# A transformer block in split fp32: the two output-gate projections as one seven-product unit, with weight sums made by accumulating transfers

## The chip, the cores and the metric

The kernel runs on one core of a Trainium2 chip. The metric is device time in microseconds (us) of one execution; lower is better. A core has TensorE (PE, matrix multiplication; its weight loads are listed as PEld), VectorE (DVE), ScalarE (ACT), GpSimd (POOL) and SyncE (SP). SP, ACT and POOL can also issue transfers (DMA). Each engine works through its own queue in order and waits there for results of the others.

## What is computed

The reference is one decoder layer with 512 tokens and a model width of 1024, in float32. The part that matters here is the combined input projection, cut into sections, and the gated linear attention (GLA) that uses two of them:

```python
h = layer_norm(x, ln_in_g, ln_in_b)
q_g, k_g, v_g, r_g, a_lr, q_lat, kv_lat, gate_logits = jnp.split(h @ w_in, offsets, axis=-1)
...
o_gla = gla_chunked(q_g, k_g, v_g, log_a)
o_gla = rms_norm(o_gla, gla_norm_g)
y_gla = (o_gla * jax.nn.silu(r_g)) @ w_o_gla
...
y_mla = merge_heads(o_mla) @ w_o_mla
return (g_gla * y_gla + g_mla * y_mla) @ w_out
```

The output gate `r_g` is 512 tokens x 1024 columns, a product of `h` (512 x 1024) with 1024 columns of `w_in`. A squared-ReLU MLP and two more layer norms follow.

## The kernel before

**Split operands.** Each float32 operand of a matmul is held as two parts: a rounded "hi" part (type fp32r) and the rest, "lo". One product is then three matmuls: hi x hi, hi x lo, lo x hi. `split` (L104) makes the parts: ACT copies to hi, DVE subtracts for lo. For weights `pump` (L157) does the same at L180 (ACT) and L181 (DVE), 128x1024 elements at a time, which is two 128-row slices of the contraction by 512 columns.

**The weight stream.** `plan` (L138) appends weight pieces to one list, `stream`, in the order of use. `pump(i)` is called before piece i is used. It issues loads from SP up to two pieces ahead (L168, into the three buffers "wraw") and splits pieces up to `ahead` ahead (1, unless the entry says otherwise). An entry can say where its parts go (`home`): "w" is the pair of double buffers "whi"/"wlo", "a" is two buffers of the general pool. An entry with `src` in place of `dmas` is not loaded by `pump`; it takes a buffer that other code has filled.

**Buffers.** `A` (L72) gives 4 KB a partition: "C" has 8 such buffers, the general tag "A" 24. `B` (L76) gives 2 KB and has 22. `MM` gives one of four accumulators for the large products, `PX` one of four for everything else. A tile that finds no free buffer waits for one.

**Products.** `gemm_fm` (L221) and `gemm_tm` (L246) loop over k, the eight 128-row slices of the contraction, and within a slice over the accumulators. After each k they call `tick`, which lets the first few of a list of generators (`active`, spawned with `spawn`) issue their next piece of work: the latents, the score levels of GLA, the GLA output. A generator's work thereby stands between the large products on every queue. The framework takes the traced order as priority and places each instruction when it finds it ready, so engines may run ahead of the traced order where their operands allow.

**The order.** After the layer norm comes the latent section `lat`, then q, k, and then `ORDER` (L288): r 0, v 0, g 0, r 1, v 1, g 2, the MLA query part, g 1, g 3, and again the query part. The index of r and v is the half of 512 columns; half 0 serves heads 0 and 1. `proj_r` (L599) computes one half: 8 slices x 4 token tiles x 3 matmuls of 128x512, at L264, L265 and L266, which `proj_v` and others use too. For each token tile it forms x (1 + tanh(x / 2)) with one Tanh on ACT (L604) and one DVE operation (L607), which both read the accumulator. `proj_v` (L588) splits its result instead.

**Background generators.** `latents2` (L548) normalises and transposes the latents. `gla_levels` (L637) builds the scores of one head in about twelve steps, alternating between DVE (L649, L685), ACT (L667) and small matmuls, with totals and products on POOL (L624, L632, L635). `gla_out` (L735) starts for a head once its scores, its value half and its r half are there. `WID` says how many generators a tick advances: 2 during q and k, 3 afterwards.

**An example elsewhere in the kernel.** The second product of the MLP (`win_f2`, L1170) already uses seven products for each 2 x 2 block of matrices, with sums of weights made on DVE (`win_sums`), and adds its results to rows in SBUF by accumulating transfers from POOL (L1216). Its weights are loaded by POOL too (L1131).

## Time and profile before

| | us |
|---|---|
| median of three runs | 880.97 (880.94 to 882.45) |
| the profiled execution | 881.23 |
| its span, first to last instruction | 879.5 |

A line of a group of instructions reads: line, engine, operation, output <- inputs, shapes, count, then busy time in us, the mean of one in ns, and the idle time of the engine just ahead of them with what ended it. A line of the timeline begins with the start and the length in us. In the table of stretches each engine has its busy time and, in brackets, the number of its instructions; then come the clock granted to PE (1.00 is full), the share of time that the DMA engines were busy, and GB/s. A line of waits reads: who waited, for whom, total us, how often, longest.

### The profile page before, as it was taken

Reading aid. Unit: us, or ns where it says so; the run is one execution under the profiler, and the core shown is the slowest. Engines: PE = TensorE matmul, PEld = TensorE weight load, DVE = VectorE, ACT = ScalarE, POOL = GpSimd, SP = SyncE. Lnnn points to the kernel's source line nnn. Section 1 sums busy time; section 2 is a strip of 40 time slices with the busy share of each in tenths; the row PEclk is TensorE's granted clock in tenths of the full one; section 3 lists DMA queues with packets and bytes.
Section 4 is the critical chain, followed back from the end, with each engine's and each line's share of the span. In section 5 each row is a group of like instructions: output and inputs, shape, how many; then the busy total and the mean of one; then the engine's idle time right before and its main releaser. Section 6 shows DMA issues by size and latency. Waiting matters only on the chain. (4 is left out here: it accounts for less than half of the span.)

```text
span 879.5 us, 11469 instructions
## 1 busy us (share of the span) xinstructions
PE 861.5 (98%) x4336; PEld 735.0 (84%) x4336; DVE 562.8 (64%) x925; ACT 443.3 (50%) x766; POOL 141.4 (16%) x184
## 2 busy tenths in 40 slices
PE   5999999999999999999999999999999999999996
PEld 5988888888888888888988888988888888888885
DVE  6934774648455244557876797886567646754697
ACT  5547462556344333345654414565357546644662
POOL 2204330211011010000000013004400520242023
PEclk9999999999999999999999999999999999999998
DMA  7513223222232323112306628006940990398075
GB/s 224 158 49 93 75 73 96 73 72 57 81 87 81 90 60 110 47 55 60 103 27 262 192 75 284 1 0 170 291 114 27 263 256 29 63 302 209 1 183 104
DMA packets 63415, 101.13 MB, mean 115 GB/s; under 512 B 7777, under 2 KB 31764, under 8 KB 63360
## 3 DMA queue, kind: packets, MB, share of 16 engines
q1 hardware_dynamic: 48400, 64.04, 23.7%
q0 software_dynamic: 13040, 32.71, 15.6%
q10 hardware_dynamic: 1920, 3.66, 1.2%
q8 instruction: 34, 0.56, 0.3%
q14 instruction: 21, 0.17, 0.1%
HBM read 82.56 MB, written 3.67 MB: 98 GB/s over the span
## 5 line engine op out<-in xcount | busy, mean ns | idle before, releaser
L181 DVE TENSOR_TENSOR wlo<-wraw,whi 128x1024 fp32r<-128x1024 f32 (+2 forms) x102 | 116.3, 1140 | 148.1 <-ACT whi L180 142.0
L231 PE MATMUL mm<-h,whi 128*128 128x512 f32 x416 | 162.4, 391 | 0.0
L232 PE MATMUL mm<-h,whi 128*128 128x512 f32 x416 | 162.3, 390 | 0.0
L233 PE MATMUL mm<-h,wlo 128*128 128x512 f32 x416 | 156.4, 391 | 0.0
L180 ACT ACTIVATE whi<-wraw 128x1024 fp32r<-128x1024 f32 (+2 forms) x102 | 99.8, 978 | 110.3 <-PE mm L232 51.5
L233 PEld LDWEIGHTS mm<-h,wlo 128*128 128x128 f32 x416 | 78.0, 188 | 16.2
L231 PEld LDWEIGHTS mm<-h,whi 128*128 128x128 f32 x416 | 78.1, 188 | 15.7
L232 PEld LDWEIGHTS mm<-h,whi 128*128 128x128 f32 x416 | 78.2, 188 | 15.5
L1216 POOL DMA_DIRECT2D res<-ev x54 | 47.7, 994 | 237.1 <-ACT ev L1214 190.9
L265 PE MATMUL mm<-wlo,h 128*128 128x512 f32 x128 | 50.5, 395 | 0.0
L266 PE MATMUL mm<-whi,h 128*128 128x512 f32 x128 | 50.1, 391 | 0.0
L264 PE MATMUL mm<-whi,h 128*128 128x512 f32 x128 | 48.2, 395 | 0.0
L1281 ACT ACTIVATE relu<-mm 128x512 f32<-128x512 f32 x32 | 18.8, 595 | 57.2 <-PE mm L233 57.2
L359 POOL TENSOR_TENSOR mv<-mv,mhalf 128x1 f32<-128x1 f32 x4 | 4.1, 1034 | 208.6 <-DVE mv L358 208.6
L649 DVE TENSOR_TENSOR qk<-qk,tot 128x512 f32<-128x512 f32 x28 | 20.1, 719 | 19.9 <-ACT M L667 19.7
L180 ACT ACTIVATE xh<-wraw 128x1024 fp32r<-128x1024 f32 (+1 forms) x20 | 19.0, 960 | 26.9 <-PE mm L266 15.3
L667 ACT ACTIVATE M<-qk 128x256 f32<-128x256 f32 x56 | 24.0, 456 | 16.9 <-DVE qk L649 16.7
L181 DVE TENSOR_TENSOR wlo<-wq,whi 128x1024 fp32r<-128x1024 f32 x15 | 18.3, 1223 | 20.4 <-ACT whi L180 20.4
L266 PEld LDWEIGHTS mm<-whi,h 128*128 128x128 f32 x128 | 24.1, 188 | 4.8
L265 PEld LDWEIGHTS mm<-wlo,h 128*128 128x128 f32 x128 | 24.1, 188 | 4.6
L264 PEld LDWEIGHTS mm<-whi,h 128*128 128x128 f32 x128 | 23.9, 188 | 4.6
L1214 ACT ACTIVATE ev<-mm 128x512 f32<-128x512 f32 x20 | 11.9, 600 | 28.8 <-DMA res<-ev 23.9
(405 smaller groups left out, 2215.1 us busy)
## 6 DMA issues: line engine op xcount, KB each, us to landing
wraw<-in_w_in_dram SPq DMA_DIRECT2D x40, 512.0 KB, 3.6
wraw<-in_w_ff_dram SPq DMA_DIRECT2D x32, 512.0 KB, 7.1
wq<-in_w_ff_dram POOLq DMA_DIRECT2D x32, 512.0 KB, 10.0
res<-ev POOLq DMA_DIRECT2D x54, 256.0 KB, 8.6
wraw<-in_w_o_gla_dram SPq DMA_DIRECT2D x8, 512.0 KB, 3.7
wraw<-in_w_o_mla_dram SPq DMA_DIRECT2D x8, 512.0 KB, 3.4
wraw<-in_w_out_dram SPq DMA_DIRECT2D x8, 512.0 KB, 4.3
wraw<-in_w_in_dram SPq DMA_DIRECT2D x8, 360.0 KB, 4.6
```

Of the source, the lines that this page charges most:

```text
L180: st["ins"] = act(hi[:, :nk, :n], raw[:, :nk, :n], AF.Copy)
L181: vtt(lo[:, :nk, :n], raw[:, :nk, :n], f(hi[:, :nk, :n]), op=ALU.subtract)
L231: mm(o, hi[:, c], xh, start=first, stop=False)
L232: mm(o, hi[:, c], xl, start=False, stop=False)
L233: mm(o, lo[:, c], xh, start=False, stop=last)
L264: mm(o, xh, hi[:, :n], start=opens, stop=False, skip_group_check=share)
L265: mm(o, xh, lo[:, :n], start=False, stop=False, skip_group_check=share)
L266: mm(o, xl, hi[:, :n], start=False, stop=last, skip_group_check=share)
L649: vtt(new, new, view(tot, o + 1, -1, 2, 0, s), op=ALU.mult)
L667: act(packed(M, s, i), half_lr(qk, s, i), AF.Copy)
L1216: nc.gpsimd.dma_start(res[tt + t][:, j * T:(j + 1) * T], e, accum_op=ALU.add)
L1281: act(r, ps, AF.Relu)
```

## The change

The two halves of r become one unit. Write `hT` (h transposed, split) as 2 x 2 blocks, tokens 0 to 255 and 256 to 511 by slices 0 to 3 and 4 to 7, and the r columns of `w_in` likewise (W11, W12 above W21, W22). Seven block products replace eight; each is 4 slices x 2 token tiles x 3 matmuls of 128x512.

Four products use a sum of weight blocks. `T1` = W12 + W11; `T2` adds W22 to it in place, `T3` adds W12 to the buffer of W22, and `T4` adds W21 to T2. The first block of each is loaded, and every further one is added, by a transfer of 512 KB that POOL issues (with `accum_op`); a block is two such transfers. W11 and W21 are loaded from SP as before. All 14 half blocks go through `pump`, split two pieces ahead, with homes alternating between "w" and "a".

Four products use a sum of token blocks (`S1` to `S4`): a new generator, `r_sums`, makes them from hi and lo of `hT` with DVE additions and subtractions, and splits them. It is spawned ahead of q. The results come together in four tiles `R`: ACT copies an accumulator out with the wanted sign (`put`), and later DVE adds or subtracts the final accumulator and the gate function follows (`last`). Some products continue in an accumulator of an earlier one, which saves additions.

`ORDER` becomes r, v 0, v 1, g 0, g 2, and the rest as before; `finish(t_lat2)` follows r, as it followed r 0.

```diff
-    ORDER = (("r", 0), ("v", 0), ("g", 0), ("r", 1), ("v", 1), ("g", 2), ("qr", 0), ("g", 1), ("g", 3), ("qr", 1))
+    ORDER = (("r", 0), ("v", 0), ("v", 1), ("g", 0), ("g", 2), ("qr", 0), ("g", 1), ("g", 3), ("qr", 1))
+    RPH = ("T1", "11", "22", "T2", "21", "T3", "T4")
+    RAHEAD, RHOME = 2, "wawawawawawaww"
...
-            PL["r", i] = plan("w_in", C_R + i * T, T)
+            for n, op in enumerate(RPH):
+                for hf in range(2):
+                    PL["r", n, hf] = len(stream)
+                    if op in ("11", "21"):
+                        plan("w_in", C_R, T, 4 * (op == "21") + 2 * hf, 4 * (op == "21") + 2 * hf + 2)
+                    else:
+                        stream.append({"src": lambda q=(op, hf): RW[q], "nk": 2, "n": T, "res": False})
+                    stream[-1].update(ahead=RAHEAD, home=RHOME[2 * n + hf])
...
+    def r_load(op, i, j, hf, add=False):
+        w = I["w_in"].rearrange("(k p) n -> p k n", p=P)
+        if not add:
+            RW[op, hf] = A([P, 2, T], F32, "rw")
+        k0 = 4 * i + 2 * hf
+        nc.gpsimd.dma_start(RW[op, hf], w[:, k0:k0 + 2, C_R + j * T:C_R + (j + 1) * T], **({"accum_op": ALU.add} if add else {}))
+    def r_add(dst, src, i, j):
+        for hf in range(2):
+            RW[dst, hf] = RW[src, hf]
+            r_load(dst, i, j, hf, add=True)
+    def r_sums():
+        H, L = slice(0, 256), slice(256, T)
...
+        for _ in range(4):
+            yield
+        X = [B([P, 2, 256], F32, "sx") for _ in range(2)]
+        RS["S1"], RS["S4"] = pair("s1"), pair("s4")
+        for m in range(2):
...
+            for kk in range(2):
+                k = 2 * m + kk
+                t = B([P, 2, 256], F32, "st")
+                vtt(t, f(hT[k + 4][:, :, L]), f(hT[k][:, :, L]), op=ALU.subtract)
+                vtt(x[:, kk], t[:, 0], t[:, 1], op=ALU.add)
+                yield
+            split(x, RS["S1"][0][:, c], RS["S1"][1][:, c])
+            yield
+            for kk in range(2):
+                k = 2 * m + kk
+                for w in range(2):
+                    vtt(x[:, kk], x[:, kk], f(hT[k][:, w, H]), op=ALU.add)
+            yield
...
+            split(y, RS["S4"][0][:, c], RS["S4"][1][:, c])
+            yield
+        RS["S2"] = pair("s2")
+        for m in range(2):
...
+            split(X[m], RS["S2"][0][:, c], RS["S2"][1][:, c], scale=-1.0)
+            yield
+        RS["S3"] = pair("s3")
...
+    def proj_r():
+        a, b = [MM() for _ in range(2)], None
+        b = [MM() for _ in range(2)]
+        R = {}
+        def put(key, t, o, scale=1.0):
+            if key not in R:
+                R[key] = A([P, 2, T], F32, "rg")
+            act(R[key][:, t], o, AF.Copy, scale=scale)
+        def last(key, t, o, op):
+            r = R[key][:, t]
+            vtt(r, r, o, op=op)
             th = B([P, T], F32, "th")
+            act(th, r, AF.Tanh, scale=0.5)
+            stt(r, th, 1.0, r, op0=ALU.add, op1=ALU.mult)
...
+        for n in range(7):
+            o = a if n in (1, 3, 5) else b
+            for hf in range(2):
+                pump(PL["r", n, hf])
+                for pp in range(2):
+                    for t in range(2):
+                        xh, xl = lhs(n, 2 * hf + pp, t)
+                        hi, lo = [w[:, pp] for w in stream[PL["r", n, hf]]["w"]]
+                        opens = n in (0, 1, 4, 6) and hf == 0 and pp == 0
+                        mm(o[t], xh, hi, start=opens, stop=False, skip_group_check=True)
+                        mm(o[t], xh, lo, start=False, stop=False, skip_group_check=True)
+                        mm(o[t], xl, hi, start=False, stop=hf == 1 and pp == 1, skip_group_check=True)
+                if hf == 0 or n == 6:
+                    tick(None)
+                if n == 0 and hf == 1:
+                    r_add("T2", "T1", 1, 1)
+                if n == 2 and hf == 1:
+                    r_add("T3", "22", 0, 1)
+                if n == 3 and hf == 1:
+                    r_add("T4", "T2", 1, 0)
+            for t in range(2):
...
+                elif n == 3:
+                    last("12", t, o[t], ALU.subtract)
+                elif n == 4:
+                    last("11", t, o[t], ALU.add)
+                elif n == 5:
+                    put("21", t, o[t])
+                    last("22", t, o[t], ALU.subtract)
+                else:
+                    last("21", t, o[t], ALU.add)
+            if n < 6:
+                tick(None)
...
     t_lat = spawn(latents())
+    t_rs = spawn(r_sums())
+    for hf in range(2):
+        r_load("T1", 0, 1, hf)
+    r_add("T1", "T1", 0, 0)
     gemm_fm(PL["q"], hT, T, ev_q)
+    for hf in range(2):
+        r_load("22", 1, 1, hf)
     t_lat2 = spawn(latents2())
     gemm_fm(PL["k"], hT, T, ev_k)
```

More of the change, by code (lines that the diff above doesn't have):

```diff
@@ L597, in proj_v @@
         gemm_tm([PL["v", hp]], hT, T, e, guard=guard)
-    def proj_r(hp):
-        rg = []
-        def e(a, j, ps):
-            th = B([P, T], F32, "th")
-            act(th, ps, AF.Tanh, scale=0.5)
-            if a % 2 == 0:
-                rg.append(A([P, 2, T], F32, "rg"))
-            stt(rg[-1][:, a % 2, :], th, 1.0, ps, op0=ALU.add, op1=ALU.mult)
-            if a == NT - 1:
-                Rp[hp] = rg
-        gemm_tm([PL["r", hp]], hT, T, e)
+    RS = {}
+    def r_load(op, i, j, hf, add=False):
[4 more added lines that the diff above has]
+        nc.gpsimd.dma_start(RW[op, hf], w[:, k0:k0 + 2, C_R + j * T:C_R + (j + 1) * T], **({"accum_op": ALU.add} if add else {}))
@@ new lines, in proj_r, with lhs @@
+    def proj_r():
[9 more added lines that the diff above has]
+            vtt(r, r, o, op=op)
+            th = B([P, T], F32, "th")
+            act(th, r, AF.Tanh, scale=0.5)
+            stt(r, th, 1.0, r, op0=ALU.add, op1=ALU.mult)
+        def lhs(n, k, t):
+            c = slice(t * P, (t + 1) * P)
+            d = slice(256 + t * P, 256 + (t + 1) * P)
+            if n in (1, 4):
+                h = hT[k + 4 * (n == 4)]
+                return h[:, 0, c], h[:, 1, c]
+            if n == 6:
+                return hT[k + 4][:, 0, d], hT[k + 4][:, 1, d]
+            key = {0: "S1", 2: "S4", 3: "S2", 5: "S3"}[n]
+            while key not in RS:
+                step(t_rs)
+            return [w[:, k, c] for w in RS[key]]
+        for n in range(7):
[19 more added lines that the diff above has]
+            for t in range(2):
+                if n == 0:
+                    put("22", t, o[t], -1.0)
+                elif n == 1:
+                    put("11", t, o[t])
+                elif n == 2:
+                    put("12", t, o[t], -1.0)
+                elif n == 3:
[9 more added lines that the diff above has]
+                tick(None)
+        Rp[0], Rp[1] = [R["11"], R["21"]], [R["12"], R["22"]]
```

28 lines of the change are left out of this document (25 added, 3 removed).

## The prediction

> **What bounds the kernel now.** I read the page's engine totals first.
>
> ```profile
> span 879.5 us, 11469 instructions
> PE 861.5 (98%) x4336; PEld 735.0 (84%) x4336; DVE 562.8 (64%) x925; ACT 443.3 (50%) x766; POOL 141.4 (16%) x184
> ```
>
> A busy share can hide waiting, since one matmul's record reaches into the next. So next: the waits of PE, all of them in the whole span.
>
> ```profile
> PE px L374 <- ACT x L363: 8.8, 1, 8.8
> PE mm L266 <- POOL h L382: 0.6, 1, 0.6
> PE mm L231 <- ACT h L377: 0.3, 1, 0.3
> PE px L374 <- DVE x L365: 0.2, 1, 0.2
> ```
>
> All four stand at the layer norms; in the input projections PE waits for nothing. Then the timeline of PE at the end of the k projection (first and last of 21 rows), and the three lines that r and v share.
>
> ```profile
> 89.83 0.39 PE L231 MATMUL mm<-h,whi 128*128 128x512 f32 x1
> ...
> 94.36 0.39 PE L233 MATMUL mm<-h,wlo 128*128 128x512 f32 x1
> ```
>
> ```profile
> L265 PE MATMUL mm<-wlo,h 128*128 128x512 f32 x128 | 50.5, 395 | 0.0
> L266 PE MATMUL mm<-whi,h 128*128 128x512 f32 x128 | 50.1, 391 | 0.0
> L264 PE MATMUL mm<-whi,h 128*128 128x512 f32 x128 | 48.2, 395 | 0.0
> ```
>
> Twenty steps in 4.53 us are 0.2265 us from start to start: the price of a 128x512 matmul. The 390 ns in the groups are records that overlap, and pricing by them would nearly double the gain. The groups hold 384 matmuls for four sections (r 0, r 1, v 0, v 1) of 96.
>
> PE is therefore the bound, dense from the first projection on. A matmul removed is worth its whole step, but only if no other engine becomes late. So the remaining views are of the other engines, where r will stand. I take 95.4 (r's first matmul) to 139.5 us, about the length the new r phase gets below.
>
> ```profile
> core 0: us, PE busy (x) PEld busy (x) DVE busy (x) ACT busy (x) POOL busy (x), PEclk, DMA share, GB/s
> 95.40:139.50 44.10, 44.10 (x226) 37.35 (x224) 33.48 (x57) 23.87 (x48) 14.14 (x21) 1.00 0.28 79
> ...
> 52.00:95.40 43.40, 43.40 (x203) 35.94 (x202) 21.08 (x31) 27.28 (x48) 11.57 (x14) 1.00 0.30 85
> ```
>
> The clock column is 1.00: the throttle is no factor.
>
> **Removed.** Two sections are 192 matmuls. The unit has 7 products x 4 pairs of k x 2 token tiles x 3 = 168. The 24 fewer are 24 x 0.2265 = **-5.44 us**. The first operand is still 128x128 and the second 128x512, so the step is the same. This is the only term that shortens anything.
>
> **Length of the r phase.** The same window, for the three matmul lines one by one:
>
> ```profile
> 95.40:139.50 44.10, 20.61 (x55) 10.24 (x55) 1.00 0.28 79
> 95.40:139.50 44.10, 21.32 (x54) 10.27 (x55) 1.00 0.28 79
> 95.40:139.50 44.10, 21.20 (x54) 10.14 (x54) 1.00 0.28 79
> ```
>
> 163 x 0.2265 = 36.9 us; the other 7.2 us of PE are the background generators (score levels, rest of the latents). The 163 matmuls saw about 14 background steps, and the new unit calls 14. So r will last 168 x 0.2265 + 7.2 = 45.3 us, 6.47 us a product.
>
> **Added on VectorE.** The window's groups:
>
> ```profile
> L181 DVE TENSOR_TENSOR wlo<-wraw,whi 128x1024 fp32r<-128x1024 f32 x7 | 8.6, 1229 | 0.9 <-ACT whi L180 0.9
> ...
> L607 DVE SCALAR_TENSOR_TENSOR rg<-th,mm 128x512 f32<-128x512 f32 x4 | 2.7, 686 | 0.9 <-ACT th L604 0.9
> ...
> L685 DVE TENSOR_TENSOR qk<-qk,g 128x512 f32<-128x512 f32 x2 | 1.4, 683 | 0.0
> ...
> L107 DVE TENSOR_TENSOR kq<-qk,kq 128x256 fp32r<-128x256 f32 x1 | 0.5, 498 | 0.0
> ```
>
> ```profile
> 95.40 0.68 DVE L685 TENSOR_TENSOR qk<-qk,g 128x512 f32<-128x512 f32 x1
> 96.00 1.22 DVE L181 TENSOR_TENSOR wlo<-wraw,whi 128x1024 fp32r<-128x1024 f32 x1
> ```
>
> The second operation starts 0.60 us after the first, whose record is 0.68 long; so one costs its record less about 0.09.
> - Weight splits: 14 instead of 8; 14 x (1.23 - 0.09) = 16.0 us.
> - Sums S1 and S4, which the first and third products need: 4 subtractions and 4 split subtractions of 128x512 (0.60) and 20 operations of 128x256 (0.41): 13.0 us. They are traced with the 16 steps of the q and k projections, where the row 52.00:95.40 shows DVE busy 21.08 of 43.40. They fit the 22.3 free, so cost 0; without that cover, 13.0.
> - S2 and S3, traced in r's first six steps: 4 subtractions and 4 splits of 128x512, 4 additions of 128x256: 6.4 us.
> - Finishing: eight tiles, each an addition from the accumulator (no row at this line; priced as L607, which reads one too) and L607's own operation: 8 x 2 x 0.60 = 9.6 us, where four tiles of one section cost 2.7 before.
>
> The background in that window is 33.48 - 7 x 1.14 - 4 x 0.60 = 23.1 us. Together 23.1 + 16.0 + 6.4 + 9.6 = **55.1 us of DVE against 45.3 of PE**. Not all of it falls inside. The first three splits run ahead of r (-3.4), the last four tiles are finished behind it (-4.8), v's first split comes in (+1.1): 48.0. S2 and S3 need only hT and may run in the same free time as S1 if buffers allow: 41.6. So DVE's demand is 41.6 to 48.0 for 45.3, and PE's loss lies between 0 and 2.7 us. That so full a DVE need not stop PE is shown further on:
>
> ```profile
> 198.00:209.00 11.00, 11.00 (x64) 9.53 (x63) 10.56 (x18) 9.13 (x19) 2.78 (x5) 1.00 0.17 48
> ```
>
> 96% busy there, and PE waited for nothing. I take **+1.0 us**, near the middle.
>
> **Added on ScalarE.**
>
> ```profile
> L180 ACT ACTIVATE whi<-wraw 128x1024 fp32r<-128x1024 f32 x7 | 7.4, 1051 | 6.9 <-PE mm L232 4.4 <-PE mm L266 2.4
> L604 ACT ACTIVATE th<-mm 128x512 f32<-128x512 f32 x4 | 2.4, 594 | 2.2 <-PE mm L266 2.0
> ```
>
> Less the same 0.09: 14 splits at 0.96, four S splits, eight copies out of the accumulators and eight Tanh at 0.50 are 23.4 us; the background is 23.87 - 7 x 0.96 - 4 x 0.50 = 15.2. Sum 38.6 of 45.3: ACT stays below DVE, and I add nothing for it.
>
> **Added transfers.** Twelve of 512 KB go through POOL's queue, eight of them accumulating; four of r's 512 KB loads stay on SP's instead of eight. For an accumulating transfer from HBM the trace has no row; the nearest are these.
>
> ```profile
> wq<-in_w_ff_dram POOLq DMA_DIRECT2D x32, 512.0 KB, 10.0
> res<-ev POOLq DMA_DIRECT2D x54, 256.0 KB, 8.6
> ```
>
> ```profile
> 600.00 1.88 POOL L1216 DMA_DIRECT2D res<-ev  x2 [52.15 <-ACT ev L1214]
> 605.71 0.86 POOL L1216 DMA_DIRECT2D res<-ev  x1 [3.83 <-DMA res<-ev]
> ```
>
> Two accumulating transfers of 256 KB, issued at 600.00, released the next one at 605.71: 5.7 us for 512 KB. A sum is two transfers of 512 KB, so between 5.7 us (if the time is latency) and 11.4 us (if it is bytes). I take 8.5. T2 is traced behind product 0 and split two weight halves ahead of product 3, T3 behind 2 for 5, T4 behind 3 for 6. Strictly in traced order T2 has from 6.5 to 19.4 - 2.3 (one split on ACT and DVE) = 17.1: 10.6 us; T3 and T4 have as much. If POOL issues as soon as the previous split has read the buffer, there are about 18. Cost 0, covered by one to two other products; at 11.4 in traced order each sum would be 0.8 us late, 2.4 in all. T1 is loaded and summed from the end of the latents on. POOL has nothing to do then:
>
> ```profile
> 67.77 6.10 POOL L545 TENSOR_TENSOR g<-g,az 128x512 f32<-128x512 f32 x4 [37.46 <-ACT az L542]
> ```
>
> Behind the waiting accumulations on POOL stand that subtraction and the totals of the score levels; only the score generator waits for those, and it now has until v 0's end, 16 us later than before (7 x 5.44 + 21.8 against 2 x 21.8 us of matmuls).
>
> [...]
>
> **Moved.** v 1 goes in front of g 0: the same 96 matmuls and four splits, its four loads earlier in SP's queue. The output generator starts a section later but takes seven steps a head, and 46 steps follow v 0. Cost 0, bounded by the buffers below.
>
> **Sum.** The profiled execution is 881.23 us: 879.5 of span and 1.7 around it. 881.23 - 5.44 + 1.0 = 876.8. The median is 0.26 below that execution, so **876.5 us**. Its own range goes from no loss (875.5) to the sum of the 2.7 and 2.4 us above on one execution (880.6).
>
> **Rivals.**
> *VectorE becomes the bound (slower).* Place: the r phase. Earlier-traced background goes first, no sum runs early, nothing is finished behind: 55.1 + 1.1 - 45.3 = 10.9 us lost, 5.5 us net, 886.4. It decides from 50.7 us of DVE work on the path (45.3 + 5.44). For it: two halves of weights are split ahead, 6.5 us of cover, and four accumulators are shared by all seven products, so a late copy holds a product. Operations with two SBUF operands can also be stretched:
>
> ```profile
> L685 DVE TENSOR_TENSOR qk<-qk,g x4: 681/1076/1782, 95.4 to 199.7; 128x512 f32<-128x512 f32 x4
> L632 POOL TENSOR_TENSOR pr<-qk x4: 1282/1297/1737, 93.5 to 194.4; 128x512 f32<-128x512 f32 x4
> ```
>
> If each of the twelve two-operand subtractions and additions of S2 and S3 met one, 0.4 us more each (1076 against 681) would be 4.8 us, and 48.0 would become 52.8. Against it: those score levels are a chain over ACT and POOL with gaps, and may slip behind r. [...] Chance 0.2.
>
> *Weight sums late.* An accumulating transfer priced as bytes and issued behind POOL's blocked work: three sums, each missing its 10.6 us window by a further POOL operation of 1.3 to 1.7 us and the 0.8: 3 x 2.5 = 7.5 us, +2.1 net, 883.0. Against it: the 18 us if issued early, and DMA only 0.28 busy. Chance 0.07.
>
> *Buffers run out.* The pool "A" has 24. In the second product: 4 raw sums, 4 qk, 5 latT, KK, S4, S2 and S3 in pairs (6), 2 rg, two splits at "a" (4): 26. An "a" split then waits for the one before it, leaving 3.2 us (half a product) for one of 2.3. A further 1 us late on each of six: 6 us, +0.6, 881.6: no change. Chance 0.07.
>
> **How the numbers follow.** Forecast 0.66, the rivals 0.2, 0.07, 0.07. This kernel's measurement cannot tell less than about 0.2% (1.8 us) from no change: faster means below 879.2. The forecast's own upper end passes that, by perhaps 0.02, and a mild form of the buffers' case is still faster (0.02): faster 0.66, no change 0.1; slower 0.24, the first two rivals less 0.03 for mild ends. Range: below, 875.2 (875.5 less the scatter of the runs); above, 884.0, which holds late sums and the first rival's lower half and leaves about 0.15 out.
>
> **What would show it.** 4312 matmuls; none of PE's waits between the latents and the output gates; 0.2265 us steps. DVE at 90% or more over r's 45 us, and PE waiting for L181 or for a copy if the 1.0 is real. T2 to T4 landing 6 to 11 us after issue, with no ACT split waiting for a DMA. Wrong if PE's waits in r exceed 3.7 us, or if they stand in v or the gates, where I put none.

## The result, and the profile after

The changed kernel takes 884.59 us (median of 8 runs, 883.13 to 885.43) and the kernel before, run beside it, 881.35 us (8 runs, 880.67 to 882.45). The ratio is 1.0032, with a 95% interval of 1.0021 to 1.0043: slower by about 0.3%, and 8.1 us above the 876.5 that was predicted. The profiled execution is the slowest of the eight (885.43 us).

The engine totals of the profile after:

```profile
span 883.7 us, 11521 instructions
...
PE 860.0 (97%) x4312; PEld 730.9 (83%) x4312; DVE 596.3 (67%) x979; ACT 456.9 (52%) x788; POOL 160.3 (18%) x196
```

The 24 matmuls are gone (4336 to 4312), and yet the span grew by 4.2 us (879.5 to 883.7). So TensorE loses some 9.6 us that it did not lose before. The waits of PE, in the whole span:

```profile
PE px L385 <- ACT x L374: 8.7, 1, 8.7
PE mm L716 <- DVE xl L181: 2.4, 1, 2.4
PE mm L715 <- ACT rg L684: 1.0, 1, 1.0
PE mm L266 <- POOL h L393: 0.9, 1, 0.9
PE px L899 <- ACT osq L903: 0.7, 1, 0.7
...
PE mm L715 <- ACT xh L180: 0.4, 1, 0.4
```

The first and the fourth stand at the layer norms, as before. Those of L715 and L716 (r's matmuls, formerly L264 to L266) are new, and so is that of L899, an output tile of the gated attention. They sum to 4.5 us, about half of what was lost; waits alone do not explain the rest. The table of stretches around r:

```profile
core 0: us, PE busy (x) PEld busy (x) DVE busy (x) ACT busy (x) POOL busy (x), PEclk, DMA share, GB/s
44.00:66.00 22.00, 22.00 (x109) 18.82 (x108) 9.78 (x18) 9.73 (x16) 0.00 (x0) 1.00 0.24 61
...
88.00:99.00 11.00, 11.00 (x51) 8.80 (x49) 10.80 (x16) 8.86 (x17) 6.96 (x9) 1.00 0.65 137
99.00:110.00 11.00, 9.58 (x47) 7.50 (x46) 11.00 (x25) 6.96 (x12) 7.10 (x9) 1.00 0.39 90
110.00:121.00 11.00, 11.00 (x58) 9.20 (x57) 11.00 (x17) 9.71 (x19) 2.40 (x2) 1.00 0.91 175
121.00:132.00 11.00, 8.55 (x41) 7.13 (x41) 10.97 (x13) 6.58 (x14) 8.32 (x10) 0.93 0.59 116
132.00:143.00 11.00, 11.00 (x52) 9.16 (x52) 10.05 (x16) 4.59 (x8) 0.00 (x0) 0.91 0.14 45
```

DVE is full from 88 to 132 us, without a microsecond of slack, while from 44 to 66 it was busy only 9.78 of 22. And the clock column is no longer 1.00: PE's clock, as a mean over 11 us, fell to 0.93 and 0.91. PE's own timeline shows where:

```profile
127.67 0.60 PE L836 MATMUL px<-M 128*128 128x128 f32 x4
130.72 0.79 PE L716 MATMUL mm<-xl,h 128*128 128x512 f32 x1 [2.45 <-DVE xl L181]
131.32 0.63 PE L717 MATMUL mm<-xh,h 128*128 128x512 f32 x1
131.74 0.63 PE L716 MATMUL mm<-xl,h 128*128 128x512 f32 x1
...
133.88 0.40 PE L715 MATMUL mm<-xh,h 128*128 128x512 f32 x1
```

After one wait of 2.45 us, seven matmuls from 130.72 to 133.88 take 3.16 us instead of 7 x 0.2265 = 1.59. In this execution the wait costs 1.6 us more than its own length. Not every wait of this length does (the last section has two, of 2.35 and 2.12 us, that did not), and perhaps not in every execution of this kernel. The granted clock, as a mean over the whole execution, is 0.995 in four of the eight (884.89 to 885.43 us) and 0.997 in the other four (883.13 to 884.28). One such spell at half clock lowers that mean by about 3.16 x 0.5 / 884 = 0.002. So I estimate that half of the executions have no such spell; only one was traced.

What had made DVE late? The operation that PE waited for, and two before it, in DVE's timeline, and beside them POOL's in the same microseconds:

```profile
97.51 2.77 DVE L107 TENSOR_TENSOR s<-sy,s 128x512 fp32r<-128x512 f32 x1
...
122.05 2.71 DVE L670 TENSOR_TENSOR st<-h 128x512 f32<-128x512 f32 x1
...
128.38 2.29 DVE L181 TENSOR_TENSOR xl<-wraw,xh 128x1024 fp32r<-128x1024 f32 x1
```

```profile
97.98 1.75 POOL L766 TENSOR_TENSOR pr<-qk 128x512 f32<-128x512 f32 x1
99.22 1.10 POOL L758 TENSOR_TENSOR tot<-tot 128x4 f32<-128x4 f32 x1
...
122.56 1.59 POOL L766 TENSOR_TENSOR pr<-qk 128x512 f32<-128x512 f32 x1
...
128.09 1.50 POOL L769 TENSOR_TENSOR qkp<-pr,qkp 128x512 fp32r<-128x512 f32 x1 [2.25 <-ACT qkp L768]
```

A 128x512 operation that otherwise takes 0.68 us took 2.77 and 2.71, and a 128x1024 one 2.29 instead of 1.22, each beside arithmetic of POOL. That is a suspicion so far; a stretched record can also be a symptom. The parts xh of that last split had been ready since 120.7 on ACT:

```profile
104.47 1.40 ACT L801 ACTIVATE M<-qk 128x256 f32<-128x256 f32 x2 [2.42 <-DVE qk L819]
...
108.07 0.45 ACT L801 ACTIVATE M<-qk 128x256 f32<-128x256 f32 x1 [0.82 <-DVE qk L783]
108.42 1.07 ACT L684 ACTIVATE rg<-mm 128x512 f32<-128x512 f32 x2
...
119.67 1.06 ACT L180 ACTIVATE xh<-wraw 128x1024 fp32r<-128x1024 f32 x1
```

The same rows show how DVE's lateness reaches PE through ACT. At 108.07 ACT stands 0.82 us before a score level whose input DVE has not finished; the copy L684, which frees an accumulator for the next product, is queued behind it, and PE waits 1.0 us for that copy.

For all runs I added up, over the matmul records, how far each start stands from the one before beyond the step of its size (the usual one in the traces: 0.2267 us for 512 columns, 0.120 for 256, 0.110 for 128, and so on); this counts waits, and slow clock too. The stretch from 88 to 154 us holds the r phase. Times are medians in us, and "before" is the range of the kernel before beside the runs. The losses are those of the one profiled execution, which is up to 1.4 us off its kernel's median (x3_plain 882.35, x19_width2 884.50), so a row's time and its sum need not match within that:

```
kernel                     time    0-62  62-88  88-154  154-250  later   sum
before                  881.1-881.5  4.6   0.1    0.2     0.6     2.1    7.5
after                     884.59   5.2   1.2    6.8     0.7     3.1   17.0
x1_order                  881.94   4.4   0.1    0.2     0.7     2.2    7.6
x2_nosums                 880.98   4.6   1.5    2.4     0.6     3.2   12.3
x3_plain                  883.79   5.0   1.2    4.2     0.7     3.2   14.2
x4_s3late                 889.96   5.6   1.2    9.9     0.6     3.2   20.5
x5_poolwrite              884.90   4.3   8.6    0.9     0.7     2.2   16.7
x7_poolsums               896.17   6.1   2.0   14.6     0.6     3.2   26.5
x10_early                 879.11   5.6   0.6    1.6     0.6     3.1   11.6
x11_lasthome              888.56   5.1   1.2    9.8     0.6     3.2   20.0
x12_poolwrite2            884.12   5.7   4.4    3.1     0.7     2.2   16.2
x13_early_pw              881.77   4.8   5.1    0.8     0.7     2.2   13.6
x14_s14early              882.81   4.6   0.6    5.1     0.6     3.1   14.1
x16_early_g0              879.73   4.6   0.6    1.6     2.0     2.2   11.0
x17_poolthin              879.84   5.2   1.9    0.3     0.7     3.1   11.1
x18_s1first               878.80   4.2   0.1    1.6     0.7     3.1    9.6
x19_width2                883.09   5.3   0.8    7.5     0.8     2.3   16.8
x21_before_thin           881.44   4.3   0.1    0.2     0.6     2.1    7.3
x22_s1first_thin          877.01   4.1   0.1    0.2     0.7     3.0    8.3
```

For the changed kernel the sum rises by 9.5 us, which with -5.44 gives +4.1 against +4.2 in the span. Of the 9.5, 6.6 stand in the r phase, 1.1 in the k projection ahead of it, 1.0 later (mostly the new wait at L899), and 0.6 at the start, which differs from kernel to kernel (4.1 to 6.1) for no reason that I found.

### The profile page after: what moved, and what is told of

Its sections match the earlier page's. It is cut to its first block, busy times and chain, and to the rows that moved or that the text cites. A ratio compares the mean times of both kernels' runs of the same rounds, so it can differ in the third digit from the quotient of the medians.

```text
span 883.7 us, 11521 instructions
## 1 busy us (share of the span) xinstructions
PE 860.0 (97%) x4312; PEld 730.9 (83%) x4312; DVE 596.3 (67%) x979; ACT 456.9 (52%) x788; POOL 160.3 (18%) x196
## 5 line engine op out<-in xcount | busy, mean ns | idle before, releaser
L181 DVE TENSOR_TENSOR wlo<-wraw,whi 128x1024 fp32r<-128x1024 f32 (+2 forms) x96 | 108.0, 1125 | 135.1 <-ACT whi L180 124.0
L231 PE MATMUL mm<-h,whi 128*128 128x512 f32 x416 | 163.0, 392 | 0.0
L180 ACT ACTIVATE whi<-wraw 128x1024 fp32r<-128x1024 f32 (+2 forms) x96 | 93.5, 974 | 88.0 <-PE mm L232 51.1
L231 PEld LDWEIGHTS mm<-h,whi 128*128 128x128 f32 x416 | 78.2, 188 | 15.7
L180 ACT ACTIVATE xh<-wraw 128x1024 fp32r<-128x1024 f32 (+1 forms) x22 | 21.1, 969 | 27.1 <-PE mm L266 15.6
L181 DVE TENSOR_TENSOR wlo<-wq,whi 128x1024 fp32r<-128x1024 f32 x15 | 18.4, 1223 | 20.4 <-ACT whi L180 20.4
L181 DVE TENSOR_TENSOR xl<-wraw,xh 128x1024 fp32r<-128x1024 f32 (+1 forms) x22 | 25.0, 1150 | 5.4 <-ACT xh L180 5.2
L1270 POOL DMA_DIRECT2D wq<-in_w_ff_dram x32 | 24.0, 813 | 10.9 <-issue 4.2
L231 PE MATMUL mm<-ogT,whi 128*128 128x512 f32 x64 | 25.7, 401 | 0.0
L265 PE MATMUL mm<-wlo,h 128*128 128x512 f32 x64 | 25.5, 398 | 0.0
L266 PE MATMUL mm<-whi,h 128*128 128x512 f32 x64 | 25.3, 395 | 0.0
L232 PE MATMUL mm<-ogT,whi 128*128 128x512 f32 x64 | 25.3, 395 | 0.0
L232 PE MATMUL mm<-omT,whi 128*128 128x512 f32 x64 | 25.2, 394 | 0.0
```

Of the source, the lines that this page charges most:

```text
L180: st["ins"] = act(hi[:, :nk, :n], raw[:, :nk, :n], AF.Copy)
L181: vtt(lo[:, :nk, :n], raw[:, :nk, :n], f(hi[:, :nk, :n]), op=ALU.subtract)
L231: mm(o, hi[:, c], xh, start=first, stop=False)
L232: mm(o, hi[:, c], xl, start=False, stop=False)
L265: mm(o, xh, lo[:, :n], start=False, stop=False, skip_group_check=share)
L266: mm(o, xl, hi[:, :n], start=False, stop=last, skip_group_check=share)
```

## Experiments

**Order and transfers: excluded.** First the new order alone, on the kernel before:

```diff
-    ORDER = (("r", 0), ("v", 0), ("g", 0), ("r", 1), ("v", 1), ("g", 2), ("qr", 0), ("g", 1), ("g", 3), ("qr", 1))
+    ORDER = (("r", 0), ("r", 1), ("v", 0), ("v", 1), ("g", 0), ("g", 2), ("qr", 0), ("g", 1), ("g", 3), ("qr", 1))
```

> The kernel before with its two old r sections, in the new order of sections (r 0, r 1, v 0, v 1, g 0, g 2, ...). Theory V (VectorE is full where the sums, the splits and the finishing operations of the new unit stand, and PE waits for it): the order alone costs nothing, 881.4 within 1 us. Theory O (the order of the sections costs, through buffers and the output generator): slower by 1 to 4 us, with PE waits behind v 0.

`x1_order`: 881.94 against 881.06 us, ratio 1.0013 (1.0002 to 1.0025), and no wait of PE that was not there before. The order costs about 0.9 us (0.2 to 2.2 by the interval).

Then the weight sums as plain loads:

```diff
-        nc.gpsimd.dma_start(RW[op, hf], w[:, k0:k0 + 2, C_R + j * T:C_R + (j + 1) * T], **({"accum_op": ALU.add} if add else {}))
+        nc.gpsimd.dma_start(RW[op, hf], w[:, k0:k0 + 2, C_R + j * T:C_R + (j + 1) * T])
```

> The changed kernel with plain transfers in place of the accumulating ones, so the weight sums are left out and the last block loaded stands in their place; as many transfers, in the same order. Theory W: 877 to 880. Theories V and B: no change, 884.6 within 1.

`x3_plain`: 883.79 us, ratio 1.0028 (1.0016 to 1.0040): 0.8 us less than the change, within the scatter of its runs, with the same waits for L181 (2.1) and L684 (0.9). Its r phase loses 4.2 instead of 6.8 us in the table, mostly because no slow clock follows the wait of 2.1 us in its profiled execution. In the changed kernel's own trace the twelve transfers land like this (four plain ones in 4.2 to 4.7 us, the eight accumulating ones in 5.8 to 7.9):

```profile
rw<-in_w_in_dram POOLq DMA_DIRECT2D x12, 512.0 KB, 5.9
```

**Token sums: the larger part.** All additions and subtractions of `r_sums` left out, one POOL memset per tile in their place; the splits stay:

```diff
-                t = B([P, 2, 256], F32, "st")
-                vtt(t, f(hT[k + 4][:, :, L]), f(hT[k][:, :, L]), op=ALU.subtract)
-                vtt(x[:, kk], t[:, 0], t[:, 1], op=ALU.add)
+                if kk == 0:
+                    nc.gpsimd.memset(x, 1.0)
...
-                vtt(y[:, kk], t[:, 0], t[:, 1], op=ALU.add)
+            nc.gpsimd.memset(y, 1.0)
```

> The changed kernel without the 32 additions and subtractions that make the token sums S1 to S4; constant values are written to the same tiles by POOL, and the splits, the buffers, the transfers and the matmuls stay. Some 14.6 us less on VectorE. Theory V: PE's waits in r fall from 7.6 to under 2 us, time 877 to 879. Theory W (late weight sums) and theory B (the 24 buffers run out): no change, 884.6 within 1.5.

`x2_nosums`: 880.98 us, 3.6 below the change, but above the 877 to 879 of theory V. The 2.4 us wait for L181 in r is gone; 2.4 us remain in r and 1.5 before it. (The memsets wait for no operand; what such memsets can disturb is shown further on.) So the sums' time on DVE matters, though the unit stays at the time of the kernel before (ratio 0.9999, 0.9989 to 1.0008) without them.

**Sums on POOL or later: worse.** The same 32 operations on POOL:

```diff
-                vtt(t, f(hT[k + 4][:, :, L]), f(hT[k][:, :, L]), op=ALU.subtract)
-                vtt(x[:, kk], t[:, 0], t[:, 1], op=ALU.add)
+                gtt(t, f(hT[k + 4][:, :, L]), f(hT[k][:, :, L]), op=ALU.subtract)
+                gtt(x[:, kk], t[:, 0], t[:, 1], op=ALU.add)
...
```

> The changed kernel with all 32 additions and subtractions of the token sums on POOL instead of VectorE; the splits stay. VectorE has 13 us less to do, POOL some 28 us more. If only VectorE's amount of work counts: 880 to 882, as without the sums. If theory P holds, POOL's reads hold VectorE's split operations in turn, and the sums come late: 884 to 892.

`x7_poolsums`: 896.17 us, ratio 1.0168 (1.0153 to 1.0183), slower than either theory had it. The stretch of r:

```profile
88.00:143.00 55.00, 45.96 (x210) 36.41 (x208) 52.70 (x66) 33.86 (x61) 48.79 (x49) 0.94 0.51 105
```

POOL is at 48.79 of 55, but DVE, with the sums taken away, is still at 52.70. In the whole span it has 32 operations less (947) and is busy 598.9 us against 596.3: what was taken off it came back as longer operations.

S3 four steps later:

```diff
+        for _ in range(4):
+            yield
         RS["S3"] = pair("s3")
```

> The changed kernel with the sum S3 (needed by the sixth product) traced four background steps later; nothing else. The same VectorE work in another order, and two pairs of buffers taken later. If the order of VectorE's queue decides (S3 ahead of the split for the fifth product), the wait of 2.6 us and the slow clock behind it go: 880 to 881. If the amount of work decides, the wait only moves: 884.6 within 1.5.

`x4_s3late`: 889.96 us, ratio 1.0109 (1.0075 to 1.0144), outside both expectations. The wait of 2.4 us at 128 us is gone; the three longest waits in and behind r are now these:

```profile
PE mm L717 <- DVE rg L690: 1.7, 1, 1.7
PE mm L717 <- ACT rg L686: 1.6, 1, 1.6
PE mm L264 <- DVE rg L690: 1.2, 1, 1.2
```

That speaks against one badly placed operation: with DVE full (53.46 of the 55 us from 88 to 143), what was put off was late at the next place.

The last half of the weights split into general buffers:

```diff
-    RAHEAD, RHOME = 2, "wawawawawawaww"
+    RAHEAD, RHOME = 2, "wawawawawawawa"
```

> The changed kernel with the last half of T4 split into the general pool instead of the double buffer w, so the first split of v 0 need not wait for the half product before. A wait of PE of 1.3 us stood there without the sums; with them it is hidden behind others. 883.5 to 885: no change that can be told, and if slower, one more sign that the 24 buffers are short.

`x11_lasthome`: 888.56 us, ratio 1.0082 (1.0067 to 1.0097), outside the expected 883.5 to 885: the old waits stay, and two of 0.4 and 0.8 us at 145 and 147 us and one before v (L264 behind DVE's finishing operation, 0.9) are added. This shows what a worse placing costs; whether the 24 buffers are short in the changed kernel itself is not shown by it.

**Sums earlier: the change becomes faster than before.** The generator's four empty first steps removed, so that the sums begin in the free time of DVE during the q projection:

```diff
-        for _ in range(4):
+        for _ in range(0):
             yield
         X = [B([P, 2, 256], F32, "sx") for _ in range(2)]
```

> The changed kernel with the sum generator started at once (its four empty steps ahead of the first sum are gone), so the sums begin in the first half of the q projection, where VectorE is idle for more than half of the time, and S3 is traced in the k projection. The same work, earlier. If the work in r's own time decides (S2 and S3, 6.4 us): 880 to 882.5. If it is the buffers, which are held longer: 884.6 or slower.

`x10_early`: 879.11 us, ratio 0.9973 (0.9964 to 0.9983), better than the 880 to 882.5 expected. Two rows of its table of stretches:

```profile
44.00:66.00 22.00, 22.00 (x109) 18.82 (x108) 13.77 (x29) 10.44 (x17) 0.00 (x0) 1.00 0.24 62
...
88.00:143.00 55.00, 54.45 (x264) 44.72 (x264) 52.76 (x82) 40.27 (x73) 28.31 (x35) 1.00 0.51 106
```

DVE does 4 us more between 44 and 66 us (13.77 against 9.78). In the r phase it is as full as ever (52.76 of 55), but PE now misses 0.55 us instead of 3.86 (in the changed kernel PE was busy 51.14 of these 55), and the clock is 1.00 throughout. S3 above all has moved forward; its subtractions, first in the changed kernel, then here:

```profile
L670 DVE TENSOR_TENSOR st<-h x4: 677/682/2706, 108.6 to 122.0; 128x512 f32<-128x512 f32 x4
```

```profile
L672 DVE TENSOR_TENSOR st<-h x4: 678/682/1374, 90.6 to 96.5; 128x512 f32<-128x512 f32 x4
```

r's first matmul stands at 96.5 and 96.4 us. S3 is finished at 104.5 us instead of 128.5, and the split of S4 that had been at 97.5 us is now at 80.1.

To learn which sums matter, S1 and S4 alone early, S2 and S3 at their old steps:

```diff
-        for _ in range(4):
+        for _ in range(0):
             yield
         X = [B([P, 2, 256], F32, "sx") for _ in range(2)]
...
+            yield
+        for _ in range(4):
             yield
         RS["S2"] = pair("s2")
```

> Of the token sums, only S1 and S4 are made four steps earlier; S2 and S3 stay at the steps that they have in the changed kernel. If the loss comes from S1 and S4 still being on DVE when r begins, this gives as much as moving all four: 878.5 to 880 us. If it comes from S2 and S3 standing inside the r phase, the gap at 128 us stays and the time is 882 to 885 us.

`x14_s14early`: 882.81 us, ratio 1.0022 (1.0011 to 1.0033): 1.8 of the 5.5 us that all four bring. Of the late sums only S3 stands inside r here (subtractions at 106.3 to 119.2 us; the splits of S2 are done by 91.3), as in the changed kernel (S2 by 93.6). So S3 inside the r phase is the larger share.

**POOL's arithmetic: is the stretching the cause?** First the arithmetic of POOL in the score levels replaced by memsets, the subtraction on GL among it:

```diff
-            gtt(GL[h], GL[h], azs[h], op=ALU.subtract)
+            nc.gpsimd.memset(GL[h], -1.0)
...
-            gtt(src, a[:, :, 0], a[:, :, 1], op=ALU.add)
+            nc.gpsimd.memset(src, -1.0)
...
-        gtt(pr, qk[:, 0, :], qk[:, 1, :], op=ALU.mult)
+        nc.gpsimd.memset(pr, 1.0)
...
-        gtt(QKP[h][1], pr, f(QKP[h][0]), op=ALU.subtract)
+        nc.gpsimd.memset(f(QKP[h][1]), 0.0)
```

> The changed kernel with POOL's arithmetic for the decay totals and the q-k products left out (constants are written instead, to the same tiles), so POOL still runs there but reads nothing from SBUF. Theory P (VectorE's operations with two SBUF operands are held by POOL's reading operations; 72.0, 73.9, 97.5, 122.0 and 128.4 us are the held ones, some 7 us in all): no VectorE addition or subtraction of 128x512 above 0.8 us in the r phase, waits of PE down by 3 to 5 us, time 879.5 to 882. Without theory P: no change, 884.6 within 1.5.

`x5_poolwrite`: 884.90 us, so the time missed. But the r phase lost only 0.9 us, and the loss had moved to the k projection:

```profile
PE mm L231 <- ACT qk L488: 5.8, 1, 5.8
```

A memset waits for no operand (the one on GL, L556, ran at 62.9 us, where the subtraction had waited for ACT until 68.4), and ACT's order changed: ahead of its copies of q (L488) stand parts of the score levels (L761) and five table loads of 1.28 us where the changed kernel has two, so the copies came late. Without these memsets that wait is 1.6 us at most in any run. The experiment disturbed what it did not mean to. The same with GL's subtraction kept, alone and with the early sums:

> The changed kernel with the arithmetic of POOL in the score levels (the pair totals, the product of q and k, its subtraction) replaced by POOL memsets of the same tiles, so the scores are not the reference's; the subtraction on GL stays. DVE has every operation that it has in the changed kernel. Theory: DVE is too full in the r phase because its operations with two SBUF operands are stretched beside POOL's arithmetic; then no such operation of the r phase is above 0.8 us, the gaps at 106 and 128 us go, TensorE's loss in 95 to 145 us falls from about 6.5 to under 1.5 us, and the time is 877 to 880 us, since the gap that the earlier run of this kind had at 70.7 us does not come without its memset on GL. Rival (the bare number of DVE's operations): both gaps stay, 883.5 to 885 us.

> The kernel with all token sums four steps earlier, and POOL's arithmetic in the score levels replaced by memsets (scores not the reference's). If lateness and stretching are two separate losses, this takes off what the earlier sums left (about 0.7 us of waits in the r phase): 877.5 to 879 us. If they are one loss (earlier sums only give DVE the slack that the stretching then uses), the r phase has no wait in either and the time is that of the earlier sums alone, 878.5 to 879.5 us.

`x12_poolwrite2` and `x13_early_pw`: 884.12 and 881.77 us. The same wait again, 2.6 and 3.2 us, so neither time can be read. In the r phase the first still loses 3.1 us, which the theory had not expected: it waits for a weight split on ACT (1.4) there.

So an edit that keeps the wait for the operands: the first column of each operation is computed, the rest of the tile filled by a memset.

```diff
-            gtt(src, a[:, :, 0], a[:, :, 1], op=ALU.add)
+            gtt(src[:, :1], a[:, :1, 0], a[:, :1, 1], op=ALU.add)
+            nc.gpsimd.memset(src[:, 1:], -1.0)
...
-        gtt(pr, qk[:, 0, :], qk[:, 1, :], op=ALU.mult)
+        gtt(pr[:, :1], qk[:, 0, :1], qk[:, 1, :1], op=ALU.mult)
+        nc.gpsimd.memset(pr[:, 1:], 1.0)
...
-        gtt(QKP[h][1], pr, f(QKP[h][0]), op=ALU.subtract)
+        gtt(QKP[h][1][:, :1], pr[:, :1], f(QKP[h][0])[:, :1], op=ALU.subtract)
+        nc.gpsimd.memset(f(QKP[h][1])[:, 1:], 0.0)
```

> The changed kernel with each arithmetic operation of POOL in the score levels (pair totals, product, its subtraction) cut to its first column, the rest of the tile filled by a POOL memset; so the scores are not the reference's. Unlike the runs with memsets alone, every operation still waits for its operands, so ACT's and DVE's order should stay near the changed kernel's and the artefact near 71 us should not come. If the stretching of DVE's two-operand operations beside POOL's arithmetic makes the loss in the r phase: no such operation above 0.9 us between 95 and 145 us, both gaps (107 and 128 us) gone, 877.5 to 880 us. If it makes about half (the gaps at 107 and 128 shrink but the next late queue shows): 880.5 to 883 us. If none: 884 to 885 us.

`x17_poolthin`: 879.84 us, ratio 0.9993 (0.9976 to 1.0009): 4.7 below the change, and the r phase lost 0.3 us instead of 6.8. POOL is no less busy in r (26.45 of the 55 us against 24.78); what it does is other. Three groups of DVE from 62 to 145 us, first in the changed kernel, then in this one:

```profile
L107 DVE TENSOR_TENSOR s<-sy,s 128x512 fp32r<-128x512 f32 x4 | 4.8, 1206 | 0.0
L670 DVE TENSOR_TENSOR st<-h 128x512 f32<-128x512 f32 x4 | 4.7, 1187 | 0.0
L181 DVE TENSOR_TENSOR xl<-wraw,xh 128x1024 fp32r<-128x1024 f32 x2 | 3.5, 1750 | 0.0
```

```profile
L670 DVE TENSOR_TENSOR st<-h 128x512 f32<-128x512 f32 x4 | 2.7, 682 | 0.0
L107 DVE TENSOR_TENSOR s<-sy,s 128x512 fp32r<-128x512 f32 x4 | 2.7, 679 | 0.0
L181 DVE TENSOR_TENSOR xl<-wraw,xh 128x1024 fp32r<-128x1024 f32 x2 | 2.4, 1218 | 0.0
```

The same ten operations take 13.0 and 7.8 us: 5.2 us of stretching, nearly all on three of them, those at 97.5, 122.0 and 128.4 us. And the stretch of r in this kernel:

```profile
88.00:143.00 55.00, 55.00 (x272) 46.13 (x271) 52.59 (x92) 42.60 (x77) 26.45 (x55) 1.00 0.54 114
```

DVE 96% busy, PE without a gap. POOL's results also come sooner here, since its thinned operations are shorter (the product of q and k at 97.98 us took 1.75 us in the changed kernel, its first column at 97.92 takes 0.21 here). But DVE did not wait for them in the changed kernel: it was busy 43.76 of the 44 us from 88 to 132, and its one idle time above 0.05 us, of 0.20, ended with ACT. The transfers are as dense as in the changed kernel (0.54 of the DMA engines' time in both), so they do not make the loss either.

The same cut in the kernel before, as a control, with its stretch behind what was expected:

> The kernel before, with POOL's arithmetic in the score levels cut to its first column and the rest filled by memsets (scores not the reference's). If the reading of POOL costs time only where VectorE has no slack, nothing changes here, since VectorE was busy 21 to 34 us of 43 to 44 us around the output gate: 880.5 to 882 us. If the cut itself saves time elsewhere, so that the 4.7 us that it brought to the changed kernel are not the r phase's, this kernel falls as well: under 879 us.

```profile
88.00:143.00 55.00, 55.00 (x276) 46.35 (x276) 37.93 (x68) 27.61 (x52) 11.37 (x44) 1.00 0.27 77
```

`x21_before_thin`: 881.44 against 881.35 us, ratio 0.9999 (0.9990 to 1.0009). There DVE has slack (37.93 of the 55 us), and POOL's arithmetic costs nothing that can be measured, though the kernel before has stretched operations too (qk, 128x512, 1.43 us at 113.4). So the 4.7 us belong to the change. The kernel with the early sums has them as well, inside r, and loses little there:

```profile
120.87 1.77 DVE L785 TENSOR_TENSOR qk<-qk,tot 128x512 f32<-128x512 f32 x1
...
124.49 1.74 DVE L821 TENSOR_TENSOR qk<-qk,g 128x512 f32<-128x512 f32 x1
```

So in these runs stretching is dear only where DVE has no room for it: the cut takes 6.5 us off the r phase of the changed kernel, nothing off the kernel before, and (below) 1.4 us where the sums are early.

**Both cures, and two smaller questions.** All sums early, and S1 finished for both halves before S4 is begun:

```diff
             split(x, RS["S1"][0][:, c], RS["S1"][1][:, c])
             yield
+        for m in range(2):
+            c = slice(2 * m, 2 * m + 2)
+            x = X[m]
             for kk in range(2):
                 k = 2 * m + kk
                 for w in range(2):
```

> The kernel with all token sums four steps earlier, and in it S1 finished for both halves of the contraction before S4 is begun (the same operations). The first product then needs nothing that is made last. If the 0.65 us of wait at 95.7 us (first product, behind the split of S1 on ACT) is a matter of that order, it goes: 878.2 to 878.9 us. If ACT's split waits for something else, 879.1 us as before.

`x18_s1first`: 878.80 us, ratio 0.9974 (0.9962 to 0.9986). The wait at the first product stayed (0.5 us of waiting, 0.65 in the reckoning of the table), so that theory fell; the k projection lost 0.1 instead of 0.6. From 879.11 the time can't be told apart. With the cut of POOL's arithmetic added:

> The kernel with all token sums four steps earlier and S1 first, with the same cut of POOL's arithmetic (scores not the reference's). If late sums and stretched operations are two ways to the same shortage of VectorE in the r phase, either cure alone is enough and both give no more than one: 878.0 to 879.5 us. If they are separate losses, both together give the forecast of the prediction: 875.5 to 877 us.

`x22_s1first_thin`: 877.01 us (four runs), ratio 0.9949 (0.9934 to 0.9964): 1.8 below the early sums with S1 first, so one cure alone is not quite enough, and at the upper end of what separate losses would give. The r phase loses 0.2 us, as in the kernel before:

```profile
88.00:143.00 55.00, 55.00 (x270) 46.12 (x269) 51.06 (x88) 41.60 (x76) 23.20 (x65) 1.00 0.51 107
```

In the r phase the cures overlap: 6.5 and 5.2 us one by one, 6.6 together. One shortage of DVE is met there in two ways; of the 1.6 us that the early sums leave in r, 1.4 go with POOL's arithmetic. The early sums with S1 first also cleared the k projection, which the cut alone did not (1.9 us lost there, then 0.1).

g 0 between v 0 and v 1 again, with the early sums:

```diff
-    ORDER = (("r", 0), ("v", 0), ("v", 1), ("g", 0), ("g", 2), ("qr", 0), ("g", 1), ("g", 3), ("qr", 1))
+    ORDER = (("r", 0), ("v", 0), ("g", 0), ("v", 1), ("g", 2), ("qr", 0), ("g", 1), ("g", 3), ("qr", 1))
```

> All token sums four steps earlier, and g 0 between v 0 and v 1, as the kernel before has it. The wait of 0.85 us at 268 us (an output tile of the gated attention, behind the square of the head's output on ScalarE) was in all variants of the changed order and not in the kernel before: if the order makes it, it goes and the time is 878.0 to 878.7 us. If not, 879.1 us as with the earlier sums alone.

`x16_early_g0`: 879.73 us, ratio 0.9988 (0.9976 to 1.0001). The wait at L899 goes (later: 3.1 to 2.2), but the output generator's small matmuls now wait from 226 us on (0.6 to 2.0). No gain.

Two generators a tick instead of three during r, sums late:

```diff
+            WID[0] = 2
             proj_r()
+            WID[0] = 3
             finish(t_lat2)
```

> The changed kernel with its sums at their late steps, but each tick inside the r phase advances two background generators instead of three, so the score levels start later and less of their work competes with the sums and splits; all operations are there, some later. If DVE's total of work traced into the r phase makes the loss, the gap at 128 us shrinks under 1 us and the time is 880 to 883 us. If only the position of the token sums makes it (they stand before the same splits either way), the gaps stay and the time is 884 to 886 us.

`x19_width2`: 883.09 us, between the two expectations. The wait at 128 us is gone, but r begins with one of 1.8 us, for DVE's copies of k, and the clock falls behind it (as a mean 0.97 from 88 to 99 us and 0.88 from 99 to 110); 7.5 us are lost in r. It tells nothing for certain: the background work is needed soon either way.

## Why the prediction was wrong

- **Removed, -5.44 us: right.** 4312 matmuls at the same step (for 512 columns 0.227 us, the median of both traces). With both cures the span is 874.6 us, 4.9 below that of before; 0.9 more lost late (mostly the wait at L899) and 0.5 less at the start make up most of the difference.
- **Transfers at 0: right.** The accumulating ones took 5.8 to 7.9 us to landing; without the accumulation the time is within 0.8 us.
- **ScalarE at 0: right as an amount, incomplete as a queue.** It was busy 36.70 of the 55 us from 88 to 143. It still made PE wait 1.4 us, standing in order behind results of DVE.
- **Order at 0: nearly right.** It cost about 0.9 us on the kernel before. But in most kernels with the changed order and the new unit the output generator of the gated attention was late by the 0.7 of L899, which was not foreseen. The order alone does not make that wait: it is absent with the order on the kernel before.
- **S1 and S4 at 0, covered by "the 22.3 free": wrong.** Much of the free time lay ahead of the sums. The generator sat out four steps and then took one step a tick, so that 12.2 us of DVE went unused from 44 to 66 us, and S4 was still split at 97.5 us, inside r. Starting S1 and S4 alone earlier gained 1.8 us, all four sums 5.5.
- **"PE's loss lies between 0 and 2.7 us. I take +1.0": the step that failed.** It measured 9.5 on the profiled execution, 6.6 of them in r (1.6 of these are the slow clock). The amount of work was judged about right: the kernel with POOL's arithmetic cut has every DVE operation at its late step, DVE 96% full, and loses 0.3 us in r. What was left out of the sum and its bounds was that DVE's operations did not keep their length: 5.2 us on ten operations, in a phase that had no room for it, because S3 was made there (108.6 to 127.8 us) and not in the earlier free time that the lower bound had hoped for. Either cure alone takes off most of the loss. I had quoted the row of the stretching (681/1076/1782 ns) and used it for a rival only. The row of 198 to 209 us (DVE 96% busy, no wait of PE) did not show that a full DVE has room for longer operations.
- **The clock was taken as fixed at 1.00.** In the profiled execution the 3.2 us behind the wait of 2.45 us ran about half as fast, 1.6 us more.
- **"Wrong if PE's waits in r exceed 3.7 us" was a blunt sign.** They sum to 3.8 us, hardly more, where the loss in r was 6.6: the list of waits holds neither the slow clock (1.6 us) nor delays such as the step of 0.34 us instead of 0.2267 behind the wait that ended at 109.05 us.

The rival "VectorE becomes the bound", given 0.2, came true in its place and its engine. Its full price was 886.4. The smaller sum in its last part, 52.8 us of DVE where 50.7 break even, would be about 883.3 on one execution and 883.0 as a median; 884.6 lies about midway. Its 4.8 us of stretching is near the measured 5.2 partly by luck: of the operations that it priced only one subtraction of S3 was stretched much (2.0 us), and the rest fell on the splits of S4 and of a weight. With memsets in place of most of POOL's arithmetic the three groups took 7.8 us instead of 13.0; whether it is POOL's reading or its computing that stretches them was not shown.

What stays open: why the output generator is late by 0.7 us at L899; which waits pull the clock down; and why the startup differs from kernel to kernel by up to 2 us.

## What to carry to other kernels

When work is added to an engine that becomes full, ask where its free time is, by stretches, and whether the generator that issues the work can reach it; an average of free time covered nothing here, with 12.2 us of DVE unused from 44 to 66 us. Where VectorE will have no slack and GpSimd computes beside it, as in r here, price VectorE's operations at the stretched length that the trace shows (128x512: 0.68 us, stretched up to 1.78 in the kernel before and 2.77 in the changed one), in the forecast itself. To test for such stretching, keep the waits of the instruction that is thinned out: bare memsets changed the order of other queues (waits of 2.6 to 5.8 us for ACT at L231) and hid the answer.

## What the hardware showed beside that

- The granted clock fell after some short waits and not after others. Beside the case above (a wait of 2.45 us, then steps of 0.43 us), a wait of 1.83 us that ended at 97.5 us in the kernel with two generators a tick was followed by steps of 0.43 us from 98.3 to 101.7 us, and one of 1.44 us there, ended at 110.5 us (with a shorter one of 0.27 behind it), by the same steps from 112.2 to 115.2 us. So 1.4 to 2.5 us of waiting were sometimes enough. Two of the slow spells lasted 3.2 and 3.4 us. But a wait of 2.35 us that ended at 143.7 us with the sums on POOL, and this one of 2.12 us with plain transfers, were followed by full speed (a clock of 1.00 from 132 to 154 us there, steps of 0.23 us here), so in these runs the length of the wait alone did not decide:

```profile
128.79 0.50 PE L716 MATMUL mm<-xl,h 128*128 128x512 f32 x1 [2.12 <-DVE xl L181]
129.12 0.39 PE L717 MATMUL mm<-xh,h 128*128 128x512 f32 x1
129.35 0.40 PE L716 MATMUL mm<-xl,h 128*128 128x512 f32 x1
```

- An operation of VectorE lost more than the length of one GpSimd instruction: L670 at 122.05 us lost 2.03 us (2.71 against 0.68), beside L766 (1.59 us) and the totals ahead of it (1.09 us) and behind it (two in 2.03 us) in POOL's queue.
- Accumulating transfers of 512 KB from HBM landed in 5.8 to 7.9 us, faster than the 10.0 and 8.6 us of the rows that had stood in for them, and slower than the 4.2 to 4.7 us of the four plain ones in the same queue.
